# A hybrid streaming-encoder trunk on one core: the order of weight loads, of the embedding products, of the last frees, and products of zeros at the start

## The chip, the cores and the metric

The kernel runs on one core of one Trainium2 chip, in one launch. The metric is device time in microseconds (us), the median of several executions. TensorE (PE) does the matrix products, ScalarE (ACT) activations and copies, VectorE (DVE) elementwise work and reductions, GpSimd (POOL) a few small operations, and SyncE (SP) issues nearly all transfers. Each engine, SyncE's queue too, works in the order in which the program gives it its instructions.

## The reference, cut to what matters

Two layers (`DEPTH` = 2) work on 256 tokens of width 1024, all in float32:

```python
for i in range(DEPTH):
    x = layer_norm(ALPHA * x + 0.5 * swiglu(x, ffn1_w_up[i], ffn1_w_down[i]), ...)   # FFN 1, D_FF = 2816
    x = layer_norm(ALPHA * x + hybrid_mixer(x, ...), ...)          # RG-LRU, GLA and FoX branches
    x = layer_norm(ALPHA * x + 0.5 * swiglu(x, ffn2_w_up[i], ffn2_w_down[i]), ...)   # FFN 2
    pe = p[i] @ ple_w_proj[i]                                       # p[i]: 256 x 256
    x = layer_norm(ALPHA * x + sigmoid(x @ ple_w_gate[i] + ple_b_gate[i]) * pe, ...)
```

The mixer projects x once; the columns go to a gated linear recurrence (RG-LRU), a gated linear attention in chunks of 64 (GLA: decays as the logarithm of a sigmoid, states, an output with a norm), a forgetting attention (FoX: the logarithm of a sigmoid, summed over the tokens, added to the logits) and three gates; three branch outputs are gated, summed and projected.

## The kernel before, in words

**Numbers in two halves.** Each float32 operand of a product is split into a high half (`hi`, an ACT copy to the format that PE multiplies) and a low half (`lo`, a DVE subtraction). A product is three products: hi by hi, hi by lo, lo by hi. XX holds x transposed in both halves (XH, XL). The two token tiles of 128 rows are t = 0 and t = 1.

**Weights.** All weights lie in one array in the order of use, cut into 440 pieces of at most 128 x 1024 elements (512 KB). `Weights.prefetch` (L183) takes the next piece: it issues its load on SyncE into one of `N_RAW` = 4 raw buffers (L200), and ACT and DVE split it (L201, L202) into one of 13 slots (`R_MAIN` = 8, and `R_EXTRA` = 5 where a scope is open). `W.free` (L213) gives a slot back and prefetches two pieces, unless `W.hold` is set; then the strings such as PA = "  V  VVV" say after which step `steps` (L411) prefetches one. `W.get` prefetches until the piece that is asked for is there. A load is thus written in the program right ahead of its own split; SyncE can run ahead of the other engines, until a load waits for a raw buffer, that is for the split four pieces earlier, or until another load in its queue waits.

**FFN.** `ffn` (L424) goes over 11 chunks of 256 columns. For a chunk, `wide_feat` makes the gate g and the up product u (two pieces each, L340 to L343; L345 copies the low part out), ACT takes Silu (L496), DVE multiplies, and `split` makes h^T in two halves (hh, hl; L276, L267). The down products (L305 to L307) lag two chunks; after the last chunk a tail does chunks 8 to 10, first for t = 0, then for t = 1, while DVE does the layer norm of t = 0. `ple_inputs` (L971) loads and splits the transposed p ahead of the tail of FFN 2.

**Norm and turn.** `Norm.finish` (L377) normalises (DVE, and POOL for the power) into XR and returns two functions, which turn XR into XX: four transposes on PE (L408) and a split. They are called after those steps of the next products that a pair names: QT = (5, 6) is after the sixth and the seventh step.

**Mixer.** `run` (L909) calls a unit (a projection of some 48 products, such as `unit_ay`) after each live generator in `running` has gone one step further, in the order in which they were added. The generators `gla_decays` (products L590, L596, L603, L608), `fox_forget` (L630 to L632, L646), `gla_gate`, `lru`, `gla_states` (L747) and `gla_out` (L784, L809) thus put their steps between the units.

**Embedding stage.** `ple` (L980) makes the four embedding products (evicted by ACT, L991), loads the gate bias bg and the fourth norm's gb, then does eight gate steps for t = 0 (turning t = 1 of the norm before, at the steps that PT names) and eight for t = 1; `finish_cols` (add, tanh L1005, multiply-add, z, statistics) takes each half of 512 columns. gb has two buffers, which the norm before still holds when the load is issued. In the second layer the last quarter pieces are done by `last_step`, and `finish` writes the output.

The start loads x transposed in four parts into two of the raw buffers, alternating with the halves of the first two pieces.

Of the kernel before, what the change touches and what calls it, by code (L numbers as in the profile page):

```python
# [46 lines left out]
PT = (0, 1)  # L47
# [112 lines left out]
class Weights:  # L160


    def __init__(self, nc, a, raw, main):
        self.nc, self.src, self.raw, self.main = nc, a["wu"], raw, main
        self.extra, self.scope = None, ()
        self.next, self.live, self.hold = 0, {}, False
        self.used = {"main": 0, "extra": 0}
# [15 lines left out]
    def prefetch(self, n=1, lo=None, cuts=1, between=lambda i: None):  # L183

        for _ in range(n):
            where = self.room()
            if where is None:
                return False
            key, _, _, _, rows, _, cols, off = PIECES[self.next]
            kt = rows // P  # L190
            raw = self.raw.tile([P, PCAP], F32, tag="raw", name=f"raw{self.next}")
            pool = self.extra if where == "extra" else self.main
            hi, lw = (pool.tile([P, PCAP], F32R, tag=x, bufs=R_EXTRA if where == "extra" else R_MAIN, name=f"{x}{self.next}") for x in ("whi", "wlo"))
            hi, lw, raw = (x[:, :kt * cols] for x in (hi, lw, raw))
            src = self.src[off:off + rows * cols].rearrange("(p n) -> p n", p=P)
            m = kt * cols // cuts
            for i in range(cuts):
                between(i)
                c = slice(i * m, (i + 1) * m)
                self.nc.sync.dma_start(raw[:, c], src[:, c])  # L200
                self.nc.scalar.activation(hi[:, c], raw[:, c], AF.Copy)  # L201
                (lo or self.nc.vector).tensor_tensor(out=lw[:, c], in0=raw[:, c], in1=hi[:, c].bitcast(F32), op=ALU.subtract)  # L202
            self.live[key] = [x.rearrange("p (k n) -> p k n", k=kt) for x in (hi, lw)] + [where]
            self.used[where] += 1
            self.next += 1
        return True
# [25 lines left out]
def build(tc, a, out):  # L232
# [96 lines left out]
    def wide_feat(key):  # L329

        s, lows = work(), work()
        for i in range(2):
            o = ps()
            hi, lo = W.get(key, i)
            for k in range(KD):
                both = XX[:, k].rearrange("p s c -> p (s c)")
                if k < KD - 1:
                    TE.matmul(o, lhsT=hi[:, k, :], rhs=both, start=k == 0, stop=False)  # L340
                TE.matmul(o[:, :T], lhsT=lo[:, k, :], rhs=XX[:, k, 0, :], start=False, stop=False)  # L341
                if k == KD - 1:
                    TE.matmul(o, lhsT=hi[:, k, :], rhs=both, start=False, stop=True)  # L343
            c = slice(i * T, (i + 1) * T)
            S.activation(lows[:, c], o[:, T:], AF.Copy)  # L345
            tt(s[:, c], o[:, :T], lows[:, c], ALU.add)
            W.free(key, i)
        return s
# [62 lines left out]
    def steps(work_list, at=(), turn=(), ahead="", inserts={}):  # L411

        for i, s in enumerate(work_list):
            s()
            for n, f in zip(at, turn):
                if n == i:
                    f()
            for f in inserts.get(i, ()):
                f()
            if ahead[i:i + 1] in ("V", "G"):  # L420
                W.prefetch(1, {"V": V, "G": G}[ahead[i]])


    def ffn(l, f, ln, hp, turn):  # L424
# [55 lines left out]
        for c in range(0 if first else 2, NCH):  # L480
# [16 lines left out]
            u = wide_feat((l, f, "u", c))  # L497
            tt(s, s, u, ALU.mult)
            hi, lo = ht(c)
            split(flat(hi), flat(lo), s)  # L500
            if LAG <= c < NCH - 1:
# [4 lines left out]
            if first and c == 3:  # L506
                late_loads()
            if c == NCH - 3:
                gb = ln_params(l, ln)
        if f == 2:  # L510
# [16 lines left out]
    def mixer(l, turn):  # L527
# [92 lines left out]
        def fox_forget():  # L620
# [15 lines left out]
            for i in range(3):  # L636
# [3 lines left out]
                if i < 2:  # L640
                    tt(fc3, fc3, part, ALU.subtract)
            yield
# [272 lines left out]
        run(lambda: unit_ax(1), gla_decays())  # L915
        run(lambda: unit_ay(0), fox_forget(), gla_gate())
# [6 lines left out]
        run(lambda: unit_cq(1), gla_out())  # L923
        run(lambda: unit_k(1))
# [45 lines left out]

    def ple_inputs(l, hp):  # L971
        raw = work()
        load(raw.rearrange("p (k c) -> p k c", k=2), a["pT"][:, l])
# [6 lines left out]
    def ple(l, turn, last):  # L980
# [4 lines left out]
        for t in range(2):  # L985
# [6 lines left out]
        W.hold = True  # L992
        for i in range(2):
            W.free((l, "pe"), i)
# [40 lines left out]
        steps([lambda x=x: step(0, *x) for x in order], PT, turn, PA)  # L1035
        W.hold = True
        turn0 = norms[0].finish(gb, last=last)
# [6 lines left out]

    def late_loads():
# [4 lines left out]
        w = zp.tile([P, D], F32, tag="z", name=nm("cst"))  # L1050
        load(w[:, :256], a["cb"])
        V.tensor_copy(flat(cb16), w[:, :256])
# [24 lines left out]
    raws = [rawp.tile([P, PCAP], F32, tag="raw", name=nm("xr")) for _ in range(2)]  # L1077

    def x_part(k):
        s = raws[k // 4][:, (k % 4) * 256:(k % 4 + 2) * 256]  # L1080
        load(s, a["xT"][:, k * 256:(k + 2) * 256])
        split(XH[:, k:k + 2, :], XL[:, k:k + 2, :], s.rearrange("p (j c) -> p j c", j=2))

    for k in (0, 4):
        W.prefetch(1, cuts=2, between=lambda i: x_part(k + 2 * i))
# [84 lines left out]
```

## Time and profile before

| what | us |
|---|---|
| median of three runs | 1316.31 (1315.8 to 1317.02) |
| the profiled execution | 1317.07 |
| its span, first to last instruction | 1315.3 |
| PE busy in the span | 1287.2 (98%) |
| DVE busy | 888.6 (68%) |
| ACT busy | 703.9 (54%) |
| POOL busy | 46.5 (4%) |

The profiled execution is 0.76 us above the median. A product is listed longer than it holds PE, since products overlap: the distance from start to start is the rate. Idle time of an engine counts only where PE, or the end, waits for it. In the windows, PEclk is the granted share of PE's clock, 1.00 for 2.4 GHz and 0.50 for 1.2 GHz; ahead of the first record it reads 1.00 whatever the clock was.

### The profile page before, as it was taken

Reading aid. Unit: us, or ns where it says so; the run is one execution under the profiler, and the core shown is the slowest. Engines: PE = TensorE matmul, PEld = TensorE weight load, DVE = VectorE, ACT = ScalarE, POOL = GpSimd, SP = SyncE. Lnnn points to the kernel's source line nnn. Section 1 sums busy time; section 2 is a strip of 40 time slices with the busy share of each in tenths; the row PEclk is TensorE's granted clock in tenths of the full one; section 3 lists DMA queues with packets and bytes.
Section 4 is the critical chain, followed back from the end, with each engine's and each line's share of the span. In section 5 each row is a group of like instructions: output and inputs, shape, how many; then the busy total and the mean of one; then the engine's idle time right before and its main releaser. Section 6 shows DMA issues by size and latency. Waiting matters only on the chain. (4 is left out here: it accounts for less than half of the span.)

```text
span 1315.3 us, 19952 instructions
## 1 busy us (share of the span) xinstructions
PE 1287.2 (98%) x7892; PEld 1134.0 (86%) x7892; DVE 888.6 (68%) x1200; ACT 703.9 (54%) x1001; POOL 46.5 (4%) x42
## 2 busy tenths in 40 slices
PE   8999999999999999999999999999999999999996
PEld 7888888999999888887778888899999988888885
DVE  6776675678658666667776667665876586666676
ACT  6655545975445455554345556359655444555541
POOL 0000000000011000000000000000000110000000
PEclk9999999999999999999999999999999999999998
DMA  8865746446556465574555557463454655555731
GB/s 268 286 195 192 242 144 209 142 146 197 168 196 208 132 204 193 188 238 158 177 192 191 191 188 250 134 227 123 158 193 156 195 194 169 189 186 190 254 129 71
DMA packets 70061, 245.47 MB, mean 187 GB/s; under 512 B 8144, under 2 KB 8784, under 8 KB 69968
## 3 DMA queue, kind: packets, MB, share of 16 engines
q1 hardware_dynamic: 69680, 243.81, 56.2%
q8 instruction: 62, 1.02, 0.3%
q10 hardware_dynamic: 288, 0.39, 0.1%
q14 instruction: 31, 0.25, 0.1%
HBM read 243.12 MB, written 1.05 MB: 186 GB/s over the span
## 5 line engine op out<-in xcount | busy, mean ns | idle before, releaser
L202 DVE TENSOR_TENSOR wlo<-raw,whi 128x1024 fp32r<-128x1024 f32 (+2 forms) x442 | 538.6, 1228 | 252.5 <-ACT whi L201 251.3
L201 ACT ACTIVATE whi<-raw 128x1024 fp32r<-128x1024 f32 (+2 forms) x442 | 457.2, 1044 | 217.2 <-PE ps L318 80.7
L340 PE MATMUL ps<-XX,whi 128*128 128x512 f32 x1050 | 373.2, 393 | 0.0
L341 PE MATMUL ps<-XX,wlo 128*128 128x256 f32 x1200 | 312.5, 281 | 0.0
L341 PEld LDWEIGHTS ps<-XX,wlo 128*128 128x128 f32 x1200 | 226.0, 188 | 12.7 <-DVE wlo L202 0.2
L340 PEld LDWEIGHTS ps<-XX,whi 128*128 128x128 f32 x1050 | 196.9, 188 | 40.0
L317 PE MATMUL ps<-XX,whi 128*128 128x256 f32 x688 | 196.6, 286 | 5.9 <-ACT whi L201 5.9
L319 PE MATMUL ps<-XX,wlo 128*128 128x256 f32 x688 | 193.0, 281 | 0.0
L318 PE MATMUL ps<-XX,whi 128*128 128x256 f32 x688 | 193.0, 281 | 0.0
L305 PE MATMUL ps<-whi,hh 128*128 128x512 f32 x368 | 145.3, 395 | 2.5 <-ACT hh L276 2.5
L307 PE MATMUL ps<-whi,hl 128*128 128x512 f32 x368 | 144.1, 392 | 0.0
L306 PE MATMUL ps<-wlo,hh 128*128 128x512 f32 x368 | 143.2, 389 | 0.0
L345 ACT ACTIVATE w<-ps 128x256 f32<-128x256 f32 x150 | 57.3, 382 | 157.6 <-PE ps L343 157.6
L305 PE MATMUL ps<-whi,XX 128*128 128x512 f32 (+2 forms) x360 | 140.6, 391 | 0.0
L307 PE MATMUL ps<-whi,XX 128*128 128x512 f32 (+2 forms) x360 | 137.6, 382 | 1.1 <-DVE XX L267 1.1
L306 PE MATMUL ps<-wlo,XX 128*128 128x512 f32 (+2 forms) x360 | 137.5, 382 | 0.0
L317 PEld LDWEIGHTS ps<-XX,whi 128*128 128x128 f32 x688 | 130.3, 189 | 8.1 <-ACT whi L201 5.9
L318 PEld LDWEIGHTS ps<-XX,whi 128*128 128x128 f32 x688 | 130.4, 189 | 0.1
L319 PEld LDWEIGHTS ps<-XX,wlo 128*128 128x128 f32 x688 | 130.2, 189 | 0.2 <-DVE wlo L202 0.2
L267 DVE TENSOR_TENSOR w<-ps,w 128x256 f32<-128x256 f32 (+1 forms) x159 | 69.1, 435 | 76.4 <-ACT w L345 76.4
L307 PEld LDWEIGHTS ps<-whi,hl 128*128 128x128 f32 x368 | 69.0, 188 | 17.0 <-DVE hl L267 1.7
L305 PEld LDWEIGHTS ps<-whi,hh 128*128 128x128 f32 x368 | 69.1, 188 | 16.4 <-ACT hh L276 4.0
(171 smaller groups left out, 1371.1 us busy)
## 6 DMA issues: line engine op xcount, KB each, us to landing
raw<-in_wu SPq DMA_DIRECT2D x430, 512.0 KB, 4.2
gb<-in_lnp SPq DMA_DIRECT2D x16, 512.0 KB, 6.1
raw<-in_wu SPq DMA_DIRECT2D x8, 280.0 KB, 5.2
xr<-in_xT SPq DMA_DIRECT2D x4, 256.0 KB, 5.0
raw<-in_wu SPq DMA_DIRECT2D x4, 256.0 KB, 5.2
XR<-in_x SPq DMA_DIRECT2D x1, 1024.0 KB, 7.5
wa<-in_lru SPq DMA_DIRECT2D x2, 512.0 KB, 4.0
w<-in_bg SPq DMA_DIRECT2D x4, 256.0 KB, 5.0
```

The lines of the kernel that those rows point to most:

```text
L201: self.nc.scalar.activation(hi[:, c], raw[:, c], AF.Copy)
L202: (lo or self.nc.vector).tensor_tensor(out=lw[:, c], in0=raw[:, c], in1=hi[:, c].bitcast(F32), op=ALU.subtract)
L267: return V.tensor_tensor(out=out, in0=in0, in1=in1, op=op)
L305: TE.matmul(o, lhsT=lh[:, k, c], rhs=hi[:, kk, :], start=start and kk == 0, stop=False)
L306: TE.matmul(o, lhsT=lh[:, k, c], rhs=lo[:, kk, :], start=False, stop=False)
L307: TE.matmul(o, lhsT=ll[:, k, c], rhs=hi[:, kk, :], start=False, stop=stop and kk == kt - 1)
L317: TE.matmul(o, lhsT=hi[:, kk, c], rhs=rhs[:, k, 0, :], start=start and kk == 0, stop=False)
L318: TE.matmul(o, lhsT=hi[:, kk, c], rhs=rhs[:, k, 1, :], start=False, stop=False)
L319: TE.matmul(o, lhsT=lo[:, kk, c], rhs=rhs[:, k, 0, :], start=False, stop=stop and kk == kt - 1)
L340: TE.matmul(o, lhsT=hi[:, k, :], rhs=both, start=k == 0, stop=False)
L341: TE.matmul(o[:, :T], lhsT=lo[:, k, :], rhs=XX[:, k, 0, :], start=False, stop=False)
L345: S.activation(lows[:, c], o[:, T:], AF.Copy)
```

## The change

Seven edits. (1) Loads are parted from splits: after each prefetch the program issues loads until four pieces beyond the one just split are on the way (`load`, `split`, `prefetch`), so these loads stand in SyncE's queue ahead of loads written later. (2) In the last chunk of an FFN the two pieces of u are freed after h^T is split, not inside `wide_feat`. (3) p is loaded at the ninth chunk (`ple_load`). (4) In the mixer the forget chain is added one unit earlier, with one more empty step ahead of its transposes, and `gla_out` one unit later. (5) In `ple`, the second tile's embedding products and the frees of their weights come after the first tile's eight gate steps, and PT becomes (4, 5). (6) The conversion of the late constants runs two chunks after their loads. (7) At the start x goes to two z buffers, the third and fourth piece are loaded at once, and PE does 19 products of zeros.

```diff
-PT = (0, 1)
+PT = (4, 5)
...
+    def load(self, cuts=1, queue=None):
+        n = len(self.raws)
+        _, _, _, _, rows, _, cols, off = PIECES[n]
+        raw = self.raw.tile([P, PCAP], F32, tag="raw", name=f"raw{n}")[:, :rows // P * cols]
+        self.raws.append(raw)
+        src = self.src[off:off + rows * cols].rearrange("(p n) -> p n", p=P)
+        return [lambda q, c=c: q.dma_start(raw[:, c], src[:, c]) for c in self.cut(n, cuts)]
...
+    def split(self, where, cuts=1, between=lambda i: None):
...
+        for i, c in enumerate(self.cut(self.next, cuts)):
+            between(i)
+            self.nc.scalar.activation(hi[:, c], raw[:, c], AF.Copy)
+            self.nc.vector.tensor_tensor(out=lw[:, c], in0=raw[:, c], in1=hi[:, c].bitcast(F32), op=ALU.subtract)
...
+    def prefetch(self, n=1):
         for _ in range(n):
             where = self.room()
             if where is None:
                 return False
...
+            while len(self.raws) <= self.next:
+                for go in self.load():
+                    go(self.nc.sync)
+            self.split(where)
+            while len(self.raws) < min(self.next + N_RAW, len(PIECES)):
+                for go in self.load():
+                    go(self.nc.sync)
         return True
...
-            u = wide_feat((l, f, "u", c))
+            u = wide_feat((l, f, "u", c), c < NCH - 1)
             tt(s, s, u, ALU.mult)
             hi, lo = ht(c)
             split(flat(hi), flat(lo), s)
+            if c == NCH - 1:
+                for i in range(2):
+                    W.free((l, f, "u", c), i)
...
+            if first and c == 5:
+                late_constants()
             if c == NCH - 3:
                 gb = ln_params(l, ln)
+                if f == 2:
+                    ple_load(l)
...
                 if i < 2:
                     tt(fc3, fc3, part, ALU.subtract)
+            yield
             yield
             yield
             o16 = psp.tile([P, 1024], BF16, tag="ps", name=nm("ps16"))
...
-        run(lambda: unit_ax(1), gla_decays())
-        run(lambda: unit_ay(0), fox_forget(), gla_gate())
+        run(lambda: unit_ax(1), gla_decays(), fox_forget())
+        run(lambda: unit_ay(0), gla_gate())
...
-        run(lambda: unit_cq(1), gla_out())
-        run(lambda: unit_k(1))
+        run(lambda: unit_cq(1))
+        run(lambda: unit_k(1), gla_out())
...
-        for t in range(2):
+
+        def products(t):
             for n in range(2):
...
-        W.hold = True
-        for i in range(2):
-            W.free((l, "pe"), i)
+
+        products(0)
         bg = [work() for _ in range(2)]
...
         steps([lambda x=x: step(0, *x) for x in order], PT, turn, PA)
+        products(1)
         W.hold = True
+        for i in range(2):
+            W.free((l, "pe"), i)
         turn0 = norms[0].finish(gb, last=last)
...
+    for i in range(2):
+        xr = zp.tile([P, D], F32, tag="z", name=nm("xr"))
+        for k, go in zip((0, 2), W.load((2, 2))):
+            s = xr[:, k * 256:(k + 2) * 256]
+            load(s, a["xT"][:, (4 * i + k) * 256:(4 * i + k + 2) * 256])
+            go(nc.sync)
+            parts.append((s, 4 * i + k))
+    for _ in range(2):
+        W.load()[0](nc.sync)
+
+    idle = flat(cb16)
+    V.memset(idle, 0.0)
+    o = ps()
+    for _ in range(19):
+        TE.matmul(o[:, :256], lhsT=idle[:, :P], rhs=idle, start=True, stop=True)
```

## Rows read from the trace of the kernel before

**Rows 1.** The page, busy time (share of the span), instructions.

```profile
PE 1287.2 (98%) x7892; PEld 1134.0 (86%) x7892; DVE 888.6 (68%) x1200; ACT 703.9 (54%) x1001; POOL 46.5 (4%) x42
```

**Rows 2.** Waits of PE: us in total, times, longest.

```profile
PE ps L317 <- ACT whi L201: 5.9, 1, 5.9
PE ps L408 <- DVE XR L270: 2.7, 2, 2.3
PE ps L784 <- ACT whi L201: 2.6, 2, 1.3
PE ps L305 <- ACT hh L276: 2.5, 3, 1.9
PE ps L307 <- DVE XX L267: 1.1, 1, 1.1
PE ps L464 <- DVE w L267: 0.7, 1, 0.7
PE ps L646 <- DVE fcat L639: 0.4, 2, 0.3
```

**Rows 3.** Timeline of the start: start, us, instruction, idle before.

```profile
8.29 0.41 PE L317 MATMUL ps<-XX,whi 128*128 128x256 f32 x1
...
12.85 2.48 DVE L202 TENSOR_TENSOR wlo<-raw,whi 128x1024 fp32r<-128x1024 f32 x2 [1.31 <-ACT whi L201]
...
14.13 0.39 PE L341 MATMUL ps<-XX,wlo 128*128 128x256 f32 x1
```

**Rows 4.** Timeline of layer 0's second FFN tail, DVE and PE.

```profile
608.69 1.23 DVE L202 TENSOR_TENSOR wlo<-raw,whi 128x1024 fp32r<-128x1024 f32 x1 [0.15 <-ACT whi L201]
609.84 0.68 DVE L267 TENSOR_TENSOR w<-w,w 128x512 f32<-128x512 f32 x1
...
608.99 0.39 PE L307 MATMUL ps<-whi,hl 128*128 128x512 f32 x1
611.23 0.50 PE L305 MATMUL ps<-whi,hh 128*128 128x512 f32 x1 [1.85 <-ACT hh L276]
```

**Rows 5.** Timeline of layer 0's mixer, ACT, DVE and PE.

```profile
246.55 0.21 ACT L577 ACTIVATE w<-s 128x16 f32<-128x16 f32 x1
...
249.83 1.28 ACT L695 ACT_TABLE_LOAD   x1
...
246.11 0.68 DVE L270 SCALAR_TENSOR_TENSOR w<-ps,w 128x512 f32<-128x512 f32 x1
...
248.08 1.02 PE L603 MATMUL ps<-w,cf 128*128 128x256 f32 x4
```

**Rows 6.** Layer 0's embedding stage: timelines, and two windows (us, busy, PEclk, DMA).

```profile
631.01 1.96 SPq L200 DMA_DIRECT2D raw<-in_wu  x4
...
627.75 0.60 ACT L991 ACTIVATE w<-ps 128x512 f32<-128x512 f32 x1 [0.76 <-PE ps L307]
629.12 0.60 ACT L991 ACTIVATE w<-ps 128x512 f32<-128x512 f32 x1 [0.77 <-PE ps L307]
...
636.77 1.06 ACT L201 ACTIVATE whi<-raw 128x1024 fp32r<-128x1024 f32 x1 [3.40 <-DMA raw<-in_wu]
...
639.01 0.68 DVE L267 TENSOR_TENSOR w<-ps,w 128x512 f32<-128x512 f32 x1
...
644.77 0.69 DVE L267 TENSOR_TENSOR w<-ps,w 128x512 f32<-128x512 f32 x1
...
651.84 0.78 PE L408 MATMUL ps<-cf,XR 128*128 128x128 f32 x4 [2.30 <-DVE XR L270]
...
637.80:652.50 14.70, 12.95 (x19) 0.99 0.56 188
...
652.20:655.60 3.40, 3.40 (x12) 2.71 (x11) 2.64 (x4) 1.33 (x2) 0.00 (x0) 0.51 0.27 81
```

**Rows 7.** Timeline of the end, PE and DVE.

```profile
1303.21 0.27 PE L307 MATMUL ps<-whi,XX 128*128 128x256 f32 x1
...
1306.06 0.41 DVE L267 TENSOR_TENSOR w<-ps,w 128x256 f32<-128x256 f32 x1
```

More of the change, by code (lines that the diff above doesn't have):

```diff
@@ L165, in __init__ @@
         self.extra, self.scope = None, ()
-        self.next, self.live, self.hold = 0, {}, False
+        self.next, self.live, self.hold, self.raws = 0, {}, False, []
         self.used = {"main": 0, "extra": 0}
@@ L181, in room, with cut @@
         return "main" if self.used["main"] < R_MAIN else None
-    def prefetch(self, n=1, lo=None, cuts=1, between=lambda i: None):
+    def load(self, cuts=1, queue=None):
[5 more added lines that the diff above has]
+        return [lambda q, c=c: q.dma_start(raw[:, c], src[:, c]) for c in self.cut(n, cuts)]
+    def cut(self, n, cuts):
+        m = PIECES[n][4] // P * PIECES[n][6]
+        if cuts == 1:
+            return [slice(0, m)]
+        at = [m * x // sum(cuts) for x in np.cumsum((0,) + cuts)]
+        return [slice(x, y) for x, y in zip(at, at[1:])]
+    def split(self, where, cuts=1, between=lambda i: None):
+        key, _, _, _, rows, _, cols, _ = PIECES[self.next]
+        kt = rows // P
+        raw = self.raws[self.next]
+        pool = self.extra if where == "extra" else self.main
+        hi, lw = (pool.tile([P, PCAP], F32R, tag=x, bufs=R_EXTRA if where == "extra" else R_MAIN, name=f"{x}{self.next}") for x in ("whi", "wlo"))
+        hi, lw = (x[:, :kt * cols] for x in (hi, lw))
+        for i, c in enumerate(self.cut(self.next, cuts)):
+            between(i)
+            self.nc.scalar.activation(hi[:, c], raw[:, c], AF.Copy)
+            self.nc.vector.tensor_tensor(out=lw[:, c], in0=raw[:, c], in1=hi[:, c].bitcast(F32), op=ALU.subtract)
+        self.live[key] = [x.rearrange("p (k n) -> p k n", k=kt) for x in (hi, lw)] + [where]
+        self.used[where] += 1
+        self.next += 1
+    def prefetch(self, n=1):
         for _ in range(n):
@@ L188, in prefetch @@
                 return False
[L189 to L205, printed above, removed]
+            while len(self.raws) <= self.next:
[5 more added lines that the diff above has]
+                    go(self.nc.sync)
         return True
@@ L327, in feat, with wide_feat @@
         return o
-    def wide_feat(key):
+    def wide_feat(key, free=True):
         s, lows = work(), work()
@@ L346, in wide_feat @@
             tt(s[:, c], o[:, :T], lows[:, c], ALU.add)
-            W.free(key, i)
+            if free:
+                W.free(key, i)
         return s
@@ L419, in steps @@
                 f()
-            if ahead[i:i + 1] in ("V", "G"):
-                W.prefetch(1, {"V": V, "G": G}[ahead[i]])
+            if ahead[i:i + 1] == "V":
+                W.prefetch(1)
     def ffn(l, f, ln, hp, turn):
@@ L968, in merge_out, with ple_load @@
         return layer_norm(1, [acc[1, 0], acc[1, 1]], gb)
+    def ple_load(l):
+        ple_in[l] = work()
+        load(ple_in[l].rearrange("p (k c) -> p k c", k=2), a["pT"][:, l])
     def ple_inputs(l, hp):
-        raw = work()
-        load(raw.rearrange("p (k c) -> p k c", k=2), a["pT"][:, l])
+        raw = ple_in[l]
         p = [hp.tile([P, 2, T], F32R, tag=x, bufs=LAG + 2, name=nm(x)) for x in ("hh", "hl")]
@@ L1042, in ple @@
         return norms[1].finish(gb)
+    late = {}
     def late_loads():
@@ L1049, in late_loads, with late_constants @@
         V.memset(mhalf, -0.5)
-        w = zp.tile([P, D], F32, tag="z", name=nm("cst"))
-        load(w[:, :256], a["cb"])
-        V.tensor_copy(flat(cb16), w[:, :256])
+        late["cb"] = zp.tile([P, D], F32, tag="z", name=nm("cst"))
+        load(late["cb"][:, :256], a["cb"])
+    def late_constants():
+        V.tensor_copy(flat(cb16), late["cb"][:, :256])
         lru_constants()
@@ L1075, in lru_constants, with x_split @@
         ts(lruc, q, -8.0, None, ALU.mult)
[L1077 to L1081, printed above, removed]
+    parts = []
+    for i in range(2):
[12 more added lines that the diff above has]
+        TE.matmul(o[:, :256], lhsT=idle[:, :P], rhs=idle, start=True, stop=True)
+    def x_split(i):
+        s, k = parts[i]
         split(XH[:, k:k + 2, :], XL[:, k:k + 2, :], s.rearrange("p (j c) -> p j c", j=2))
-    for k in (0, 4):
-        W.prefetch(1, cuts=2, between=lambda i: x_part(k + 2 * i))
+    for i in range(2):
+        W.split("main", (2, 2), lambda j: x_split(2 * i + j))
     def in_scope(i):
```

## The prediction

> **What bounds the kernel now.** I read the busy table first: TensorE (PE) is busy 1287.2 of 1315.3 us [rows 1]. So the kernel can only get shorter where PE stands still, where it runs at its lower clock, or behind its last product. The waits of PE come next [rows 2]: one before the first product (5.9) and 10.0 us in eleven stops later; the reader is to see which producer is named in each. Then the timelines around each stop [rows 3 to 6], the windows with the granted clock [rows 6], and the end [rows 7]: PE starts its last product at 1303.21, and the VectorE (DVE) takes up the last gate only at 1306.06. In the eleven PE waits for work that DVE or ScalarE (ACT) does late because something less urgent stands ahead of it in the same in-order queue. The products themselves are not changed.
>
> A stop costs more than its idle time. Two products stand 2.24 apart (608.99 and 611.23) where 0.23 is usual (six products between two evictions 1.37 apart [rows 6]), so the loss is 2.01 where the wait says 1.85 [rows 4]: I add 0.16 per stop.
>
> **The start.** The first stop of 5.9 us is the landing of x and of the first weights. The order of those loads stays, so it stays. The products after it are at the lower level of the clock: 0.41 us long at 8.29 [rows 3] against 0.27 for the same shape at the end [rows 7], that is 1.2 and 2.4 GHz. The nineteen zero products (256 columns each, so some 0.2 apart at the lower level, 4 us in all) fit ahead of 5.9 and would bring the rise forward; each product that then finds the upper level is about 0.1 cheaper. But PE must then wait for the third weight piece: its second half is made by DVE from 12.85 to about 14.09 and PE uses it at 14.13 [rows 3]. Only an earlier landing of that piece helps. Its load no longer waits for a buffer that held x, so it is issued sooner, but it stands behind eight other loads. Bounds 0 and 1.2 (one split's time on DVE, 2.48 for two [rows 3]); I take **0.4**, nearer to nothing because eight loads in front of it share the same DMA engines.
>
> **h^T before the last weights.** Four FFN tails exist. In the worst, DVE works on a weight split at 608.69 (1.23 us), then on the gate product at 609.84; ACT's h^T follows, and PE, ready at 608.99 + 0.23, starts at 611.23 [rows 4]. With the two frees behind the h^T split, the two splits that stood in front of it (2.4 us on DVE, and ACT's waits for their data) fall behind it. The gate product moves to about 607.4, h^T to 608.7, ahead of PE's need at 609.2. What is late instead are pieces of the next stage's weights, which PE reaches only after the rest of this tail, the second tile's tail and the norm between them (twelve pieces of 1.37, 16 us): cover enough, and gone only if a split came 16 us late. The wait named L305 is 2.5 in three stops [rows 2]; plus 3 x 0.16; plus the products after each stop, which come slowly because h^T's low half is late too (0.50 long instead of 0.39 at 611.23), about 0.3 in each of four tails. Together 4.1; bounds 2.5 and 4.3. I take **4.1**.
>
> **The mixer: two stops go, one comes.** L784 (GLA output) waits 2.6 in two stops and L646 0.4 in two [rows 2], one of each per layer. Both wait for DVE work behind others. The output moves a unit (5.6 us of products) later, more than its 1.3; the forget chain's cumulative sums move a unit earlier, and the transposes stay. So 3.0 + 4 x 0.16 = 3.6 is had back, up to 4.6 if the state products stop halting inside their own group.
>
> But the forget chain starts a unit earlier, and its Abs, Exp and Ln go to ACT's queue earlier too. They take ACT from 246.55 to 249.83, two table loads included [rows 5]. ACT is full there, without a gap. Moved ahead of the tanh of the gate, they push everything behind them back by 3.28: the tanh, two weight splits and, through DVE's half of these splits, the stt at 246.11 that makes log alpha (ready 246.79). PE takes that at 248.08 (L603, four products). After: ready at 246.79 + 3.28 = 250.07, so PE waits **2.0 in each of two layers**, 4.0. What is queued behind that instruction on PE (the next projection) is late by the same; ACT gains by it, since from 249.83 on its work is what it was. Bounds: no wait, if ACT gets there 3 us sooner for another reason; 3.3, if the slack of 1.3 is gone. Net: 3.6 to 4.6 less 4.0; I take **0.3**.
>
> The Trainium skill speaks against this move: "ScalarE: Activation LUTs", section on what a table load costs, gives each switch about 1.3 us and as much again for a drain. The rows have three calls of 0.21 and two loads of 1.28 in 3.28 us, which leaves no room for drains [rows 5]. By the page's sum of about 2.7 per switch the block would be some 6.0 and the wait 4.7 a layer, 5.5 us more in all. The same page, section on table sets, has one set with both exp and ln; then one load would do and the wait would be 0.7.
>
> **The embedding stage of layer 0.** SyncE's queue is in order, and the loads of gb for the fourth norm wait until the third norm has let its buffers go. Weight loads behind them go out from 631.01; the first split starts at 636.77 where ACT had waited 3.4 for it, the gate's first add on DVE is behind it at 639.01 and the second at 644.77 [rows 6]. From then on DVE is the bound (12.95 busy of 14.70), PE waits for XR until 651.84, and the clock falls to its lower level for 3.4 us (0.51 granted) [rows 6].
>
> After: the loads are issued four pieces ahead, before bg and gb, so the split at step 2 finds its data. The second tile's products, 2 x 1.37 = 2.74 us [rows 6], go behind the first tile's gate: PE's total is the same, the first tile's sums are ready 2.74 sooner. The first tile's own embedding products end 1.37 before the eviction at 627.75, at 626.4; eight gate steps of 1.37 and two turns of 0.45 (four transposes each) end at 638.3. From the second add to XR it took 651.84 - 644.77 = 7.07; with 1.3 for a split in front XR is there at 646.7. PE asks for it at 649.5 (651.84 less the 2.30 that it waited). So that stop goes (2.46 with its extra), and with it the fall of the clock, 3.4 x 0.5 = 1.7, of which some products were waiting anyway: 1.6. Behind it stand L307 1.1, the second L408 0.4, L464 0.7 [rows 2], with extras 2.7. DVE's work is not less, PE arrives some 5 us sooner, and DVE's lead of 5 us is spent by then: I leave 2.2 of them. The sum is 2.46 + 1.6 + 0.5 = **4.6**; bounds 2.5 (a stop of 1.5 stays at the turn) and 6.8 (all goes). bg is now issued behind weight loads that wait for splits, so it lands later; the first four gate steps (5.5 us) hide it, and if it is later than they are, the first add is late by as much, with 2.8 to spare before PE asks. Moving pT's load ahead holds one of twelve work buffers for two chunks, in which eight others are taken: nothing, unless a buffer ran short, when a chunk's gate would wait for one.
>
> **The end.** In layer 1 the same late split held DVE, and from the first gate to the end DVE never caught up: PE ended at 1303.49, the last add began at 1306.06 [rows 7]. With the first tile's gate done earlier (split not late, 2.74 sooner), DVE needs about 2.2 per last quarter and keeps pace; the add follows PE's end at once. Gain 1306.06 - 1303.55 = **2.5**; bounds 1.0 and 2.5. The 9.2 us behind it are unchanged.
>
> The late constants (two chunks later) end no wait of PE [rows 2] and are first used in the mixer, after the whole first FFN: nothing.
>
> **Sum.** 0.4 + 4.1 + 0.3 + 4.6 + 2.5 = 11.9. The profiled execution took 1317.07 (span 1315.3); 1305.2 after. It lies 0.76 above the median of three, 1316.31; so the forecast for the median is **1304.4 us**.
>
> **Rivals.** *No wait at L603* (ACT has room, or one table load serves Exp and Ln): 1.3 to 4.0 less, about 1300.6 to 1303. For it: the slack before was 1.3 already. Against: the rows stand back to back on ACT, and 1.3 does not hold 3.28. Chance 0.17. *DVE stays the bound in the embedding stages:* the turn still waits in layer 0 and the end gains 1.0 only, and one h^T still waits for a late landing: 3 to 5 more, 1307.5 to 1309.5. For it: 12.95 of 14.70 busy. Chance 0.17. *A dearer move on ACT:* the block costs 6.0 there instead of 3.28, by waits between its calls that its old place hid; a wait of 4.7 a layer, 1309.9, and so long a stop would let the clock fall as the 2.3 stop did [rows 6]. Against: its parts fill the 3.28 to within 0.1. Chance 0.04. The page's sum above gives the same. *Slower:* the mixer's own small loads now stand behind weight loads that wait for splits. The add of the forget bias (bf) stands in DVE's queue ahead of the convolution and of the splits; if bf lands late, DVE stops there, ACT's Abs with it, and log alpha too. The gain other than the mixer's is 11.6, so it decides when log alpha comes not at 250.1 but 6 us later, 256, in both layers; from there each us costs two, and at 259 the time is some 1322. Against: four weight loads at most stand in front of it, and the first group of eight b pieces lies between. Chance 0.03. *The change does nothing that counts*, because each producer is late for a second reason: within 0.2% (what a measurement of this kernel can tell from no change, 2.6 us): 0.02. The forecast: 0.57.
>
> **From that the numbers.** The likeliest is 1304.4; its own terms give 1300.5 to 1308. The range that leaves 0.2 out: 1299.5 to 1308.5. Faster by over 0.2% (below 1313.7): 0.94; within: 0.03; slower: 0.03.
>
> **What would show it.** Right: L305, L784, L646 and the long L408 gone from PE's waits; a new wait at L603 for DVE, about 1.9 idle, twice; granted clock unbroken at the turn of the layers; first product at about 5.9, second half of the third piece used near 13.8; last add within 0.1 of PE's end. Wrong: no L603 wait (1300); a wait of PE on a weight split in the first gate (13 pieces held at once, the embedding's two among them); a wait of DVE for bg; a start later than 5.9.

## The result, and the profile after

The changed kernel takes 1303.65 us (median of four runs, 1301.51 to 1304.82) where the one before takes 1316.59 beside it (1315.8 to 1317.02): a ratio of 0.9908, 95% interval 0.9893 to 0.9924, faster by 0.9%. The forecast was 1304.4. The profiled execution of the changed kernel took 1304.82, span 1303.0, the uppermost of its four. Its line numbers are higher: L208 and L209 are the halves of the weight split (L201, L202 before), L326 to L328 the products L305 to L307, L338 to L340 the products L317 to L319, L632 the decay sums (L603), L814 the GLA output (L784), L430 the turn (L408), L1133 the zero products; L190 issues the weights, L285 the other loads (L200, L264), and the helpers' lines L288, L291, L297 are L267, L270, L276 of before.

The page after, busy time [rows 1]:

```profile
PE 1287.5 (99%) x7911; PEld 1136.4 (87%) x7911; DVE 889.4 (68%) x1201; ACT 703.9 (54%) x1001; POOL 46.6 (4%) x42
```

The waits of PE after (us in total, times, longest) [rows 2]:

```profile
PE ps L632 <- DVE w L291: 3.5, 2, 1.8
PE ps L1133 <- DVE cb L1130: 1.0, 1, 1.0
PE ps L362 <- DVE wlo L209: 0.5, 1, 0.5
PE ps L486 <- DVE w L288: 0.5, 1, 0.5
PE ps L340 <- DVE wlo L209: 0.5, 2, 0.2
PE ps L430 <- DVE XR L291: 0.4, 1, 0.4
PE ps L338 <- ACT whi L208: 0.3, 1, 0.3
```

The eleven stops of before are down to two short ones (L486, L430). New are three at the start, 1.0 together (L340, L362), and the entry that counts, the decay sums.

Where the time came from is read by setting the same product in both traces side by side; the difference of its start times is PE's lead there, and the step from one such product to the next is what that stage gave:

| product | before | after | lead | step |
|---|---|---|---|---|
| first low half of the third weight piece | 14.13 | 14.10 | 0.03 | 0.03 start |
| first of mixer 0 | 222.84 | 221.81 | 1.03 | 1.00 FFN 1 of layer 0 |
| first of FFN 2, layer 0 | 459.13 | 456.98 | 2.15 | 1.12 mixer 0 |
| fourth after h^T in its tail | 612.30 | 607.75 | 4.55 | 2.40 FFN 2 |
| first of layer 1 | 683.92 | 673.79 | 10.13 | 5.58 embedding stage 0 |
| first of mixer 1 | 876.01 | 865.08 | 10.93 | 0.80 FFN 1 of layer 1 |
| first of FFN 2, layer 1 | 1112.21 | 1103.37 | 8.84 | -2.09 mixer 1 |
| end of PE's last product | 1303.49 | 1294.24 | 9.25 | 0.41 FFN 2 (0.00 in the embedding stage) |
| end of the span | 1315.29 | 1303.02 | 12.27 | 3.02 behind PE |

**Start** [rows 3]. Timeline of PE and DVE after:

```profile
1.04 4.23 PE L1133 MATMUL ps<-cb 128*128 128x256 bf16 x19 [1.04 <-DVE cb L1130]
5.55 0.58 PE L338 MATMUL ps<-XX,whi 128*128 128x256 f32 x1 [0.27 <-ACT whi L208]
...
12.83 2.50 DVE L209 TENSOR_TENSOR wlo<-raw,whi 128x1024 fp32r<-128x1024 f32 x2 [1.01 <-ACT whi L208]
...
14.10 0.38 PE L362 MATMUL ps<-XX,wlo 128*128 128x256 f32 x1 [0.48 <-DVE wlo L209]
```

The zero products fit, the first product comes at 5.55 instead of 5.90 and the clock is up at 6.07 instead of 10.53; but the third piece's second half is begun at 12.83 (12.85 before) and PE waits for it. Its load was issued at 4.48 instead of 7.39, but ACT, which waits for the landing, can begin its half at 11.73, as before (11.76). All of the lead is gone at 14.10.

**h^T** [rows 4]. Timeline of layer 0's second tail after, DVE, ACT, PE:

```profile
604.13 0.69 DVE L288 TENSOR_TENSOR w<-w,w 128x512 f32<-128x512 f32 x1
...
606.47 2.36 DVE L209 TENSOR_TENSOR wlo<-raw,whi 128x1024 fp32r<-128x1024 f32 x2 [0.26 <-ACT whi L208]
...
604.85 0.63 ACT L297 ACTIVATE hh<-w 128x512 fp32r<-128x512 f32 x1 [1.62 <-DVE w L288]
...
607.07 0.39 PE L326 MATMUL ps<-whi,hh 128*128 128x512 f32 x1
```

The gate product no longer has a split in front of it; the two splits (606.47) are behind, and PE starts without a stop, 1.6 after the high half is made. Set on the clock of before (2.15 more), the gate product comes at 606.3; I had said 607.4.

**Mixer** [rows 5]. Timeline of ACT, DVE and PE after:

```profile
239.16 0.20 ACT L606 ACTIVATE w<-s 128x16 f32<-128x16 f32 x1
239.38 1.28 ACT L607 ACT_TABLE_LOAD   x1
...
240.91 1.28 ACT L608 ACT_TABLE_LOAD   x1
...
242.42 1.28 ACT L799 ACT_TABLE_LOAD   x1
...
244.78 1.99 ACT L208 ACTIVATE whi<-raw 128x1024 fp32r<-128x1024 f32 x2
...
245.85 2.36 DVE L209 TENSOR_TENSOR wlo<-raw,whi 128x1024 fp32r<-128x1024 f32 x2 [6.10 <-ACT whi L208]
248.13 0.68 DVE L291 SCALAR_TENSOR_TENSOR w<-ps,w 128x512 f32<-128x512 f32 x1
...
248.96 1.10 PE L632 MATMUL ps<-w,cf 128*128 128x256 f32 x4 [1.75 <-DVE w L291]
```

A window behind the stop of layer 1 (us, busy of PE, PEld, DVE, ACT and POOL, PEclk, DMA share, GB/s):

```profile
893.53:900.36 6.83, 6.83 (x20) 5.57 (x20) 1.54 (x2) 6.78 (x12) 2.20 (x2) 0.50 0.17 62
```

The forget chain's three calls and two table loads fill ACT from 239.16 to 242.42, 3.26. The tanh's load, two weight splits, DVE's halves of them and the stt for log alpha at 248.13 follow in that order, and PE stands for 1.75 (its last product in front starts at 246.93, 2.03 earlier where 0.12 is usual, so 1.91 is lost). In layer 1 the same stop is followed at 893.53 by 6.83 us at the lower level of the clock (1.2 GHz, 0.50 granted); in layer 0 of this execution it is not.

**Embedding stage** [rows 6]. Timeline of SyncE's queue, ACT, DVE and PE after:

```profile
620.91 0.89 SPq L285 DMA_DIRECT2D w<-in_bg  x2
624.68 1.65 SPq L285 DMA_DIRECT2D gb<-in_lnp  x2
...
622.31 1.05 ACT L208 ACTIVATE whi<-raw 128x1024 fp32r<-128x1024 f32 x1
...
627.41 0.69 DVE L288 TENSOR_TENSOR w<-ps,w 128x512 f32<-128x512 f32 x1 [0.31 <-PE ps L328]
...
641.13 1.41 DVE L291 SCALAR_TENSOR_TENSOR XR<-z,s,gb 128x512 f32<-128x512 f32 x2
...
657.55 0.66 PE L430 MATMUL ps<-cf,XR 128*128 128x128 f32 x4 [0.38 <-DVE XR L291]
```

The window that was shown of before, now:

```profile
637.80:652.50 14.70, 14.70 (x68) 11.77 (x67) 13.14 (x19) 6.13 (x9) 0.92 (x1) 1.00 0.45 147
```

ACT splits the piece for the second gate step at 622.31, while gb is still stuck; at the first add it is DVE that waits (0.31, for PE's sums), the clock stays up, and PE is busy throughout the window.

**End** [rows 7]. Timeline of PE and DVE after:

```profile
1293.96 0.27 PE L328 MATMUL ps<-whi,XX 128*128 128x256 f32 x1
...
1294.27 0.42 DVE L288 TENSOR_TENSOR w<-ps,w 128x256 f32<-128x256 f32 x1
```

The last add begins 0.03 behind PE's end (2.57 before).

### The profile page after: what moved, and what is told of

Read it like the earlier page. It is cut to its first block, busy times and chain, and to the rows that moved or that the text cites. A ratio compares the mean times of both kernels' runs of the same rounds, so it can differ in the third digit from the quotient of the medians.

```text
span 1303.0 us, 19990 instructions
## 1 busy us (share of the span) xinstructions
PE 1287.5 (99%) x7911; PEld 1136.4 (87%) x7911; DVE 889.4 (68%) x1201; ACT 703.9 (54%) x1001; POOL 46.6 (4%) x42
## 4 chain that ended last, share of the span: by engine, by line
PE 46%; DVE 2%; ACT 1%; issue 1%; DMA 0%; DVEq 0%; ACTq 0%
PE ps L361 9%; PE ps L326 6%; PE ps L328 6%; PE ps L327 6%; PE ps L362 5%; PE ps L338 4%; PE ps L339 4%; PE ps L340 4%; PE ps L364 1%; DVE wlo L209 1%; DVE z L291 0%; PE ps L430 0%; DMA raw<-in_wu 0%; DVE w L288 0%; DVE w L291 0%
## 5 line engine op out<-in xcount | busy, mean ns | idle before, releaser
L209 DVE TENSOR_TENSOR wlo<-raw,whi 128x1024 fp32r<-128x1024 f32 (+2 forms) x442 | 538.8, 1228 | 244.0 <-ACT whi L208 242.2
L208 ACT ACTIVATE whi<-raw 128x1024 fp32r<-128x1024 f32 (+2 forms) x442 | 458.2, 1044 | 214.8 <-PE ps L339 95.7
L362 PE MATMUL ps<-XX,wlo 128*128 128x256 f32 x1200 | 312.5, 281 | 0.5 <-DVE wlo L209 0.5
L362 PEld LDWEIGHTS ps<-XX,wlo 128*128 128x128 f32 x1200 | 226.0, 188 | 13.3 <-DVE wlo L209 0.8
L338 PE MATMUL ps<-XX,whi 128*128 128x256 f32 x688 | 195.8, 285 | 0.4 <-ACT whi L208 0.3
L340 PE MATMUL ps<-XX,wlo 128*128 128x256 f32 x688 | 192.3, 280 | 0.5 <-DVE wlo L209 0.5
L326 PE MATMUL ps<-whi,hh 128*128 128x512 f32 x368 | 144.8, 394 | 0.0
L328 PE MATMUL ps<-whi,hl 128*128 128x512 f32 x368 | 143.7, 390 | 0.0
L326 PE MATMUL ps<-whi,XX 128*128 128x512 f32 (+2 forms) x360 | 141.3, 393 | 0.0
L328 PE MATMUL ps<-whi,XX 128*128 128x512 f32 (+2 forms) x360 | 138.1, 384 | 0.0
L338 PEld LDWEIGHTS ps<-XX,whi 128*128 128x128 f32 x688 | 129.4, 188 | 3.4 <-issue 1.4
L340 PEld LDWEIGHTS ps<-XX,wlo 128*128 128x128 f32 x688 | 129.3, 188 | 1.1 <-DVE wlo L209 1.1
L288 DVE TENSOR_TENSOR w<-ps,w 128x256 f32<-128x256 f32 (+1 forms) x159 | 68.8, 435 | 80.3 <-ACT w L366 76.5
L328 PEld LDWEIGHTS ps<-whi,hl 128*128 128x128 f32 x368 | 69.0, 188 | 15.4
L327 PEld LDWEIGHTS ps<-wlo,hh 128*128 128x128 f32 x368 | 69.1, 188 | 14.7
```

Of the source, the lines that this page charges most:

```text
L209: self.nc.vector.tensor_tensor(out=lw[:, c], in0=raw[:, c], in1=hi[:, c].bitcast(F32), op=ALU.subtract)
L288: return V.tensor_tensor(out=out, in0=in0, in1=in1, op=op)
L326: TE.matmul(o, lhsT=lh[:, k, c], rhs=hi[:, kk, :], start=start and kk == 0, stop=False)
L327: TE.matmul(o, lhsT=lh[:, k, c], rhs=lo[:, kk, :], start=False, stop=False)
L328: TE.matmul(o, lhsT=ll[:, k, c], rhs=hi[:, kk, :], start=False, stop=stop and kk == kt - 1)
L338: TE.matmul(o, lhsT=hi[:, kk, c], rhs=rhs[:, k, 0, :], start=start and kk == 0, stop=False)
```

## The experiments

The ratios are to the kernel before on the same chip. Leads are worked out as in the table above.

**The loads, undone.** The changed kernel without the four pieces ahead:

```diff
             self.split(where)
-            while len(self.raws) < min(self.next + N_RAW, len(PIECES)):
-                for go in self.load():
-                    go(self.nc.sync)
```

> The changed kernel with each load written right ahead of its own split again (only the two extra loads of the start stay). My theory: the loads behind gb go out when the third norm frees it, so the split of the last gate pieces waits for its data in both layers as before, DVE starts the gate some 4 us late, the stop at the turn of layer 0 comes back at least in part and the end loses 1 to 2: 4 to 7 us slower than the changed kernel, 1307.5 to 1310.5. Rival (moving the products is enough): within 1 of 1303.65.

Measured: 1316.65 (1313.49 to 1318.16), ratio 1.0001, interval 0.9991 to 1.0011. All of the gain is gone; I had expected a part. Its PE waits between 600 and 700 us (line numbers from L223 on are three lower than in the changed kernel: L323 to L325 are the products L326 to L328):

```profile
PE ps L325 <- DVE XX L285: 1.7, 1, 1.7
PE ps L323 <- ACT whi L208: 1.3, 1, 1.3
PE ps L324 <- DVE wlo L209: 0.8, 1, 0.8
PE ps L323 <- ACT XX L294: 0.5, 1, 0.5
```

The timeline of its SyncE queue and ACT there:

```profile
629.63 20.09 SPq L190 DMA_DIRECT2D raw<-in_wu  x8
...
635.52 1.06 ACT L208 ACTIVATE whi<-raw 128x1024 fp32r<-128x1024 f32 x1 [10.20 <-DMA raw<-in_wu]
```

The weights again go out behind gb, at 629.63, ACT waits 10.2 for one, and now PE stops for the weights themselves. The embedding stage gives -1.73 instead of 5.58, with two falls of the clock of 3.4, the last FFN with its embedding stage -0.87 instead of 0.41, and the part behind PE 1.39 instead of 3.02. The other three stages of h^T keep their steps (1.01, 2.40, 0.80). So without the early loads the other edits of the embedding stage bring nothing. The profiled execution, 1314.83, is among the shorter of the ten.

**The order of the embedding products, undone** (both tiles' products first, PT as before, loads still ahead):

```diff
-PT = (4, 5)
+PT = (0, 1)
...
         products(0)
+        products(1)
+        W.hold = True
+        for i in range(2):
+            W.free((l, "pe"), i)
...
-        products(1)
         W.hold = True
-        for i in range(2):
-            W.free((l, "pe"), i)
```

> The changed kernel with the embedding products of both tiles ahead of the gate again and the turn at steps 0 and 1; loads stay four ahead. My theory (both parts give: the early load frees DVE by 3.4 us or more, the move by 2.74): DVE's chain ends 2.7 later but mostly still ahead of PE; 1 to 3 us slower than the changed kernel, 1304.5 to 1306.5, about 1 of it at the end. Rival (the move is what counts, the load was late only because PE was): 5 us slower or more, 1308.5. Other rival (the load alone): no difference, 1303.65.

Measured: 1307.63 (1306.43 to 1308.48), ratio 0.9936, interval 0.992 to 0.9952; 4.0 above the changed kernel and 1.1 above my range. Its new wait:

```profile
PE ps L328 <- DVE XX L288: 1.7, 1, 1.7
```

In the profiles the embedding stage of layer 0 gives 3.64 (5.58), with this wait beside the 0.4 at the turn, and the part behind PE 2.08 (3.02): 2.9 together. The two profiled executions are 3.2 apart; the mixers make 0.5 of it (-1.51 together against -0.97), and their stops and falls of the clock differ between executions. Whether this part is the edit's is not shown.

**h^T behind the weights again:**

```diff
-            u = wide_feat((l, f, "u", c), c < NCH - 1)
+            u = wide_feat((l, f, "u", c))
...
-            if c == NCH - 1:
-                for i in range(2):
-                    W.free((l, f, "u", c), i)
```

> The changed kernel with u's pieces of the last chunk freed inside the up product again, so that their weights' splits stand ahead of h^T. My theory: the waits for h^T come back in three tails, 2.5 idle and some 1.5 in slower products after them; 3.5 to 4.5 slower than the changed kernel, 1307 to 1308.5. Rival (loads four ahead already remove the waits for data that held ACT there): 1 slower at most.

Measured: 1308.97 (1307.15 to 1311.26), ratio 0.9951, interval 0.9936 to 0.9965; 5.3 above the changed kernel, 0.5 above my range. PE waits for h^T again:

```profile
PE ps L326 <- ACT hh L297: 3.2, 3, 1.4
```

The four steps of h^T are -0.96, 0.96, 0.70 and -1.11 in place of 1.00, 2.40, 0.80 and 0.41: 5.0 less.

**The mixer edit alone,** put into the kernel before:

```diff
             yield
             yield
+            yield
             o16 = psp.tile([P, 1024], BF16, tag="ps", name=nm("ps16"))
...
-        run(lambda: unit_ax(1), gla_decays())
-        run(lambda: unit_ay(0), fox_forget(), gla_gate())
+        run(lambda: unit_ax(1), gla_decays(), fox_forget())
+        run(lambda: unit_ay(0), gla_gate())
...
-        run(lambda: unit_cq(1), gla_out())
-        run(lambda: unit_k(1))
+        run(lambda: unit_cq(1))
+        run(lambda: unit_k(1), gla_out())
```

> The kernel before with the mixer's part of the change alone (forget chain a unit earlier with an empty step more, GLA output a unit later). My theory: waits at the GLA output and at the forget transposes gone (3.0 idle), a wait of 1.75 idle at the decay sums in each layer, and a fall of the clock behind it in some runs (1.7 to 3.4 each): between 2.5 faster and 3 slower than before, nearer to no change. Rival (the mixer's part is a gain of its own): 3 or more faster, 1313.

Measured: 1315.65 (1311.22 to 1318.88, ten runs), ratio 0.9999, interval 0.9986 to 1.0012: nothing. Its PE waits at the decay sums and at the turn:

```profile
PE ps L603 <- DVE w L270: 3.5, 2, 1.8
PE ps L408 <- DVE XR L270: 3.2, 2, 2.9
```

Two windows, behind the stops at the decay sums:

```profile
251.44:258.27 6.83, 6.83 (x20) 5.57 (x20) 1.50 (x2) 6.78 (x12) 2.24 (x2) 0.50 0.21 72
906.80:910.21 3.41, 3.41 (x10) 2.67 (x9) 0.00 (x0) 3.38 (x7) 1.17 (x1) 0.50 0.08 34
```

The mixers give -2.01 and -0.52; without the falls of the clock (half of 6.83 and of 3.41) it is 1.40 and 1.19. One reading I had not looked for: this kernel has no wait for h^T, though that edit is not in it. PE comes to the tail of layer 0 2.2 later, DVE makes the gate product at 609.87 against 609.84 [rows 4], and the stage gives back 2.15. The time of h^T was set there by the landing of the weights (ACT waits for three pieces in front of it, 1.37, 1.01 and 0.26 us), not by PE; 2 us lost ahead of that tail cost the kernel before nothing.

**The forget chain's calls on ACT a unit later,** its sums where they were:

```diff
             yield
+            yield
             lf, e = abs_log1p(fv, 16)
             yield
             stt(lf, fv, 0.0, e, ALU.min, ALU.subtract)
             yield
-            yield
```

> The changed kernel with the forget chain's Abs, Exp and Ln one step later, behind the next unit's Gelu on ACT as before the change; its sums stay a unit earlier. My theory (these calls, put ahead of the tanh and of two weight splits, make the wait at the decay sums): that wait of 1.75 idle goes in both layers, with it the lower clock that follows it in some runs; 1303.65 less 3.8 and less 1 to 2 for the clock, 1298.5 to 1300, and the runs lie closer together. Rival (ACT is the bound of the mixer's first half, and its time is owed somewhere): the wait comes back at the forget transposes or at the GLA output, and the time stays within 1 us of 1303.65.

Measured: 1310.31 (1308.81 to 1311.89), ratio 0.9957, interval 0.9942 to 0.9971: slower than the changed kernel, a miss. Its longest wait of PE:

```profile
PE ps L659 <- DVE w L291: 7.7, 2, 4.2
```

The timeline of DVE in front of it, in layer 0:

```profile
255.82 2.36 DVE L209 TENSOR_TENSOR wlo<-raw,whi 128x1024 fp32r<-128x1024 f32 x2 [8.70 <-ACT whi L208]
```

The decay sums don't wait now. But the stt that ends the forget chain is written a unit behind its Ln, and so behind two weight splits, for which DVE waits 8.7. The forget sums (L659) pay for it, and the clock falls for 6.8 us at both stops, each time before PE goes on. I had moved one half of the chain and not looked at what the other half then stands behind.

**The same with the stt right behind the Ln,** the sums two steps later:

```diff
             yield
-            lf, e = abs_log1p(fv, 16)
             yield
+            lf, e = abs_log1p(fv, 16)
             stt(lf, fv, 0.0, e, ALU.min, ALU.subtract)
             yield
             yield
```

> The changed kernel with the forget chain's Abs, Exp and Ln one step later on ACT, and the DVE step that makes the log of them in the same step, so that DVE does it before the next two weight splits; the sums stay a unit earlier than before the change. What the run with the three calls alone showed (wait gone at the decay sums, but 4.2 at the forget sums, since that DVE step stood behind two splits) should go too. My theory (both waits are places in the in-order queues of ACT and DVE, not a lack of time on them): no wait of PE over 0.6 in the mixers, no fall of the clock in them, 1297.5 to 1299.5. Rival (ACT owes the time somewhere): 1303 or more, with a wait at the forget transposes, the GLA states or the output.

Measured: 1298.86 (1297.89 to 1299.33), ratio 0.9872, interval 0.9857 to 0.9887. All its waits of PE:

```profile
PE ps L1133 <- DVE cb L1130: 1.0, 1, 1.0
PE ps L338 <- ACT whi L208: 0.8, 1, 0.8
PE ps L340 <- DVE wlo L209: 0.7, 3, 0.2
PE ps L486 <- DVE w L288: 0.6, 1, 0.6
PE ps L362 <- DVE wlo L209: 0.6, 1, 0.6
PE ps L430 <- DVE XR L291: 0.4, 1, 0.4
```

The timeline of PE at its GLA output in layer 0:

```profile
286.64 1.10 PE L814 MATMUL ps<-gs,bq 64*64 64x128 f32 x32
```

No stop is left in the mixers, no fall of the clock, and the runs lie within 1.4 us (3.3 in the changed kernel). It is 4.8 below the changed kernel, and the intervals of the two do not touch. The mixers give 2.92 and 2.78: what the edit is worth without its stop.

**The forget chain at its old place,** the output still late:

```diff
-        run(lambda: unit_ax(1), gla_decays(), fox_forget())
-        run(lambda: unit_ay(0), gla_gate())
+        run(lambda: unit_ax(1), gla_decays())
+        run(lambda: unit_ay(0), fox_forget(), gla_gate())
```

(and without the extra empty step.) 

> The changed kernel with the forget chain at its old place, GLA output a unit later as in the change. My theory: the decay sums do not wait, the forget transposes wait 0.3 to 0.4 in both layers as before; 1298 to 1300.5, some 0.8 slower than the run with the log made whole in one step. Rival: as there, 1303 or more.

Measured: 1302.33 (1300.35 to 1304.77), ratio 0.9905, interval 0.9889 to 0.9922. The profiled run (1300.35) came as expected, the median 1.8 above it. Its mixers give 1.49 and 1.41; much of what lacks to the 2.9 and 2.8 of the kernel above goes into a new wait, at FoX's products for DVE:

```profile
PE ps L859 <- DVE gv L288: 2.1, 2, 1.1
```

**The output at its old place,** the forget chain early:

```diff
-        run(lambda: unit_cq(1))
-        run(lambda: unit_k(1), gla_out())
+        run(lambda: unit_cq(1), gla_out())
+        run(lambda: unit_k(1))
```

> The changed kernel with the GLA output put back at its old place, a unit earlier; the forget chain stays early. My theory: the stop of 1.75 at the decay sums leaves VectorE and ScalarE that much lead, so the wait of TensorE at the GLA output (1.3 in each layer before) comes back only in part, 0 to 0.6 a layer: 1303.5 to 1305. Rival: the two have nothing to do with each other, the output waits 1.3 plus 0.16 in each layer again and its own products come slower as before: 1306.5 to 1308.5.

Measured: 1305.45 (1304.95 to 1305.79), ratio 0.9919, interval 0.9902 to 0.9935. That is 0.5 above my range, and between it and the rival's. No wait at the output; that at the decay sums is 3.5 as in the changed kernel. The mixers give -1.99 and 1.04, the first with a fall of the clock of 6.83 (3.41 lost): 1.42 without it. So with the stop in front, moving the output bought nothing that these runs can tell; whether it was the stop or the early loads that gave DVE and ACT the lead that the output needs, no run tells apart.

**No zero products** (the only work left out; the output does not depend on it):

```diff
-    idle = flat(cb16)
-    V.memset(idle, 0.0)
-    o = ps()
-    for _ in range(19):
-        TE.matmul(o[:, :256], lhsT=idle[:, :P], rhs=idle, start=True, stop=True)
```

> The changed kernel without the 19 products of zeros. My theory (the third weight piece's landing and split set when the second chunk of products can begin, and the low half is used at 14.1 either way): no change, 1303.65 within 1; products at 5.6 to 10 are on the lower clock level again. Rival (the earlier rise of the clock is worth what it shortens): up to 2 us slower.

Measured: 1305.08 (1304.44 to 1306.16), ratio 0.9919, interval 0.99 to 0.9937; it overlaps that of the changed kernel, though the median is 0.4 above my range. The third piece's low half is used at 14.83, 0.7 later; but the first product, which no zero products precede, also comes 0.7 later (6.25, released by ACT's high half of the weights). What the zero products are worth is not told apart from that.

**The third piece in two halves,** added to the best kernel so far (forget_log_whole), load and split:

```diff
-            self.split(where)
+            self.split(where, (2, 2) if self.next == 2 else 1)
...
-    for _ in range(2):
-        W.load()[0](nc.sync)
+    for go in W.load((2, 2)) + W.load():
+        go(nc.sync)
```

> The kernel forget_log_whole (1298.9), with the third weight piece loaded and split in two halves at the start; the bytes are the same. My theory: behind the first products TensorE waits for the low half of the third piece, which VectorE begins at 12.8 only when the whole piece has landed (11.7) and ScalarE has made its high half; with half a piece at a time the low half is ready sooner, so the products that use it begin 0.5 to 0.9 us before 14.10, and the time is 1298.0 to 1298.4. Rival: the queued bytes set it; the halves land one after the other, the second no sooner than now, the products of the second half wait in place of the first, and the time stays at 1298.9.

Measured: 1298.15 (1297.5 to 1298.95), ratio 0.9864, interval 0.985 to 0.9879. DVE and PE at the start:

```profile
11.18 2.01 DVE L209 TENSOR_TENSOR wlo<-raw,whi 128x512 fp32r<-128x512 f32 x3
...
13.91 0.28 PE L362 MATMUL ps<-XX,wlo 128*128 128x256 f32 x1
```

The low half is begun ahead of 12.83 and PE no longer waits for it. The product comes at 13.91, 0.2 before the changed kernel and 0.5 before its own base (14.42). It is the fastest measured, by 0.7 over its base, though the intervals of the two overlap, and in its profiled execution the clock rose only at 10.26 (4.35 in the base's).

The early load of p and the later conversion of the constants were not undone by themselves; what they are worth is not shown.

## Why the prediction was right, point by point

The forecast was right as a whole. The sum of its terms, 11.9, stands against 12.27 in the profiled execution (1317.07 - 1304.82 = 12.25), but all five terms were off, in both directions: -0.4, +0.5, -1.3, +1.0 and +0.5. That they cancel is luck; what held is the order of the work in the stages of h^T, in the embedding stage and at the end.

**Start: 0.4, measured 0.03.** The chosen step, an earlier landing of the third piece, did not happen: its load was issued 2.9 earlier and its second half begun at 12.83 against 12.85. The lower bound was the answer. That the piece stands behind the bytes of eight others, as I had it, fits; no run moves it ahead of them.

**h^T: 4.1, measured 1.00 + 2.40 + 0.80 + 0.41 = 4.6,** above the upper bound of 4.3. The order of the work came as written: h^T ahead of the splits, and nothing later that waits for them. Undoing it cost 5.3 in the median, 5.0 by the steps. But this gain is not a fixed price: mixer_alone shows that the stop shrinks by what PE loses ahead of it.

**Mixer: 0.3, measured 1.12 - 2.09 = -1.0.** It was a difference of two large numbers, and both carried an error. The stop was read rightly: 2.0 a layer by 3.28 on ACT less a slack, measured 1.91, 1.75 of it idle. The gain was mis-sized: forget_log_whole, which has no stop, gives 2.92 + 2.78 = 5.7 where I had 3.6 and at most 4.6. From the product in front of the GLA output's group to the one behind it it was 281.96 to 285.56 before and is 286.44 to 287.67 there, 3.60 against 1.23: besides the listed 1.3 and its 0.16 the group had halted inside itself for some 0.9 a layer, 1.8 in both where my bound left 1.0. Before, DVE and PE:

```profile
283.11 0.48 DVE L756 COPY gs<-ps 128x128 f32<-128x128 f32 x2
...
283.54 2.10 PE L784 MATMUL ps<-gs,bq 64*64 64x128 f32 x32 [1.30 <-ACT whi L201]
```

The list names ACT's split for this stop, but the products read gs, the states, which DVE begins to copy at 283.11, behind two splits of its own (280.84, 2.35), and goes on making while the group runs: the reading that they wait for DVE fits. What I left out was the clock. I named its fall only behind the longer stop of a rival, and it fell behind this one, for 6.83 us in layer 1, 3.41 lost. With these sizes the sum is 5.7 - 3.8 - 3.4 = -1.5; the 0.5 to the measured -1.0 stays open. That loss is not in every execution: the four runs go from 1301.51 (mean granted clock 0.998) to 1304.82 (0.995), and a fall of 6.83 is 3.41 / 1303 = 0.0026 of that mean.

The page that spoke against the move, the Trainium skill's "ScalarE: Activation LUTs" (section on what a table load costs, a drain with each switch), is not borne out: the block took 3.26 with two loads of 1.28 and three calls of 0.2, and the wait is 1.75 and not 4.7. Nor did one load serve exp and ln, as its section on table sets would have it: both are there, at 239.38 and 240.91.

**Embedding stage: 4.6, measured 5.58.** The steps held. XR was to be there at 646.7 less the 4.55 that PE was ahead by then, 642.2; it was there at 641.13 + 1.41 = 642.5. The stop at the turn, the fall of the clock and the wait at L307 are gone; of the last stops 1.2 stay (0.4 and 0.5 idle, 0.16 each) where I had left 2.2, and that is the difference. loads_at_split shows what carries it: without the early loads the stage gives -1.73. The order of the products gives 1.9 of the 5.6 and 0.9 behind PE.

**End: 2.5, measured 3.02.** DVE keeps pace, the add comes 0.03 behind PE: 2.54. The other 0.5 lies behind the output's first issue (1299.18, before 1310.95), from where it is 3.84 to the end instead of 4.34. The output's transfers land 2.0 to 2.1 behind their issue in both; what follows the last landing is shorter, and no run here shows why. mixer_alone has 4.34 as well, the other kernels 3.82 to 4.22.

Of the rivals none came as a whole. The one with no wait at the decay sums (1300.6 to 1303) is about the time of forget_old_place, which has no such wait but has another. The changed kernel's median lies 0.75 under the forecast, and two of its four runs show a higher granted clock (0.998, 0.997) than the profiled one (0.995). That the falls of the clock in the mixers come with the stops at the decay and forget sums is shown by the three kernels without such a stop (forget_log_whole, third_piece_halves, forget_old_place): none of them has a fall there. Why one execution falls and another doesn't stays open.

## What to carry to other kernels

Move a chain of small calls as a whole: each engine's part has its own queue, and the part left behind (here one stt behind two splits) sets the new time. A load that waits for its buffer stops every load behind it in the queue, so issue ahead of it what the engines need meanwhile; here, without that, the other edits together gave nothing. And price a stop of TensorE with what its clock does after it, and by what the next stage would have absorbed: in layer 1 a stop of 1.9 us came with 3.4 lost to the clock, and in mixer_alone 2.0 lost ahead of an FFN's tail cost nothing.

## What the runs showed of the hardware

**The clock behind short stops.** In seven of these traces PE stops at the decay sums in both layers, for 1.75 to 2.2 us. Behind eight of those fourteen stops the granted clock goes to 0.50, five times for 6.83 us and three times for 3.41; behind the other six it stays at 1.00. The stop of 1.85 in the kernel before [rows 4] had no fall behind it, and I had taken that for the rule.

**Zero products and the clock.** Without them the clock rose at 10.53, 11.73 and 12.51; with them between 3.90 and 6.07 in eight of nine traces and at 10.26 in one; in output_old_place it rose at 5.01 and was down again from 8.42 to 11.84. What the early rise is worth these traces do not tell: where it came early and held, the third piece's low half was used at 13.68 to 14.42, and otherwise, with whole pieces, at 14.13 to 15.25, but there the first product too came later (5.90 to 6.74 against 5.55 to 5.88).
